# Two casts held behind a copy, gate sums and gate condition in longer runs of column products

## The chip, the core and the metric

The kernel runs on one core of one Trainium2 chip. The core has five engines that run beside each other and wait for each other through semaphores: TensorE (PE; PEld is its loading of weights), VectorE (DVE), ScalarE (ACT), GpSimd (POOL) and SyncE (SP), which here issues DMA transfers. Products are accumulated in banks of PSUM; everything else lies in SBUF or, between stages, in DRAM. The metric is the device time of one execution in microseconds, the median of several runs.

## The reference

One layer of a hybrid decoder, in float32, for a prompt of 1024 tokens and 8 samples of 4 tokens each, model width 1024:

```python
mod = jax.nn.silu(c) @ w_ada + b_ada
shift, scale, gate = jnp.split(mod, 3, axis=-1)
h = rmsnorm(x, g_norm) * (1 + scale[:, None, :]) + shift[:, None, :]
(mq, mk, mv, mi, mf, mo, mz, aq, ak, av, az, gm, ga) = split_in(h @ w_in)
y_m, C, n, m = mlstm_branch(mq, mk, mv, mi, mf, mo, mz, C0, n0, m0, b_i, b_f, g_mn)
o = sink_attend(q, k, v, q_pos, k_pos, sinks)
y_a = o * jax.nn.silu(az)
u = jax.nn.sigmoid(gm) * (y_m @ w_mo) + jax.nn.sigmoid(ga) * (y_a @ w_ao)
x = x + gate * (u @ w_o)
```

followed by a final rmsnorm. The outputs are the normed rows, the mLSTM state (C, n, m) and the kept keys and values, for prompt and samples. Three pieces of this matter here. The *gate sums* are the columns mi and mf of `h @ w_in`, 8 columns in all. The *gate condition* is the third part of `silu(c) @ w_ada`, called `gate`. The *job mk of head 0* is 128 columns of mk.

## The kernel before

**Exact products.** A float32 operand of the large products is split into hi and lo parts of a faster type (fp32r): `split4` (line 549) makes hi with an ACT copy, which the profile calls CAST, and lo with a DVE subtraction. A product is then three: hi x hi, hi x lo, lo x hi. Small products stay in plain float32 and are done on 32 columns of the array at a time: `mm(..., share=4)`, whose outputs go to the partitions 0, 32, 64 and 96 of one bank, four products beside each other. The profile shows full products as 128\*128 and column products as 128\*32.

**Jobs and pieces.** `job` (line 607) multiplies one block of 128 columns of the weights with all 1056 tokens, in three pieces of 384, 384 and 288 tokens (`PIECES`). Each piece is 24 products into one bank of the pair `pg` (`piece`, line 561), after which `evac` copies the bank out, on ACT for the jobs aq, mq and mk. With two banks, a piece has to wait for the copy of the piece two before it. At its start a job splits the weights of the next one (`prefetch`, which calls `split_weights`) and loads those of the one after that. The order is ak, av, aq0 to aq3, mq0, mk0, mv0, mq1; the other mLSTM jobs and all later ones are done in pairs by a scheme with fewer products, and there `split4` is called without `split_weights`. So the only job whose name begins with mk and which `split_weights` sees is mk0, at the start of mq0, when the three pieces of aq3 have been written down.

**Order.** Every PE instruction is chained to the one before it, so PE works in the order in which the program is written. On ACT and DVE (`S` and `V`, objects of the class `Ordered`, line 223) the same holds during the first stage, up to `V.on = S.on = False` (line 1985). After that the compiler's scheduler lays out each engine's order from the dependencies; `no_sync` adds a dependency that only fixes an order. Every engine runs its own queue in order. `Side` (line 113) is a planner, run while the program is written: it keeps a clock in estimated microseconds of PE work (`side.now`), and between products of a job it lets generators of side work take a step. A step ends with `yield lag, banks`: how long until the next visit, and which banks that needs.

**The stage around the gate sums** (lines 1925 to 1976). ak and av are made together, `pair` after `pair`, with four groups of two k blocks. In the last group, q = 3, stand: pair of pieces 0, its copies (`pair_end`), then the gate products for tokens 0 to 511 (`gate_piece(wg, zg, 0)`: 8 column products into the bank gg0, one ACT copy to zg0); pair of pieces 1, its copies, the first four sums (`gate_sums`: four small full products that add up the four partition groups of zg0 into gp), gate products 1; pair of pieces 2, its copies, sums four to seven from zg1, and gate products 2 for the 32 sample tokens. The ninth sum and all that depends on gp come later, as side work (`gates`). After that aq0 begins.

**The gate condition** is side work, `ada_gate` (line 1990). For each half of 512 columns it loads eight blocks of weights (adar_ga), and in two visits makes four column products each (`ada_products`, line 374); then DVE adds the bank's four groups to gb, and SP stores gb to DRAM.

Of the kernel before, what the change touches and what calls it, by code (L numbers as in the profile page):

```python
# [15 lines left out]
ALU = mybir.AluOpType  # L16
# [16 lines left out]
KT = D // 128  # L33
# [151 lines left out]
def body(tc, a):  # L185
    nc = tc.nc
    with ExitStack() as ctx:
# [34 lines left out]

        class Ordered:
            def __init__(self, eng, name):
                self.eng, self.name, self.on, self.late, self.before = eng, name, True, False, None

            def __getattr__(self, op):
                f = getattr(self.eng, op)

                def call(*args, **kw):  # L230
                    ins = f(*args, **kw)  # L231
                    i = getattr(ins, "ins", ins)
                    if self.on:
                        in_order(ins, self.name)
                    elif self.late and self.before is not None:
                        no_sync(i, [self.before])
                    self.before = i
                    return ins
                return call

        @contextmanager
        def not_before(*engs):
            for e in engs:
                e.late = True
            yield
            for e in engs:
                e.late = False

        V, S, G = Ordered(nc.vector, "V"), Ordered(nc.scalar, "S"), Ordered(nc.gpsimd, "G")
        G.on = False  # L250
# [302 lines left out]
            return hi, lo  # L553

        def split_weights(raws, name, eng):
            parts = [split4(raw, f"{name}_{i}", eng) for i, raw in enumerate(raws)]
            return tuple((lambda k, w=w: w[k // 4][:, k % 4]) for w in zip(*parts))

        banks = [pg]
# [1 line left out]
        def piece(w, rh, rl, kn, name, p, evac):  # L561
            wh, wl = w
            c0, n = PIECES[p]
            banks.append(banks.pop(0))
            acc = banks[-1]([128, 384], f"g_{name}{p}")
            o = acc[:, :n]
            for k in range(kn):
                mm(o, wh(k), rh(k, c0, n), start=(k == 0), stop=False)
                mm(o, wh(k), rl(k, c0, n), start=False, stop=False)
                mm(o, wl(k), rh(k, c0, n), start=False, stop=(k == kn - 1))  # L570
                if k < kn - 1:
                    side.tick()
            evac(p, acc, c0, n)
            side.tick()

        hs = {}

        def h_hi(k, c0, n, x="h"):
            ks = k
# [839 lines left out]
        class Pair:  # L1419
# [21 lines left out]
            def samples_end(self):  # L1441
                self.kind.samples(self, halves_sum(self.sums))

            def first_sums(self, behind=None):
                self.raw["s1"] = raw_tile("ws1")
                V.tensor_tensor(self.raw["s1"], self.raw[1, 0], self.raw[1, 1], op=ALU.add)
                if behind is not None:
                    no_sync(V.before, [behind])
                V.tensor_tensor(self.raw[1, 0], self.raw[0, 0], self.raw[1, 0], op=ALU.subtract)
                V.tensor_tensor(self.raw[0, 0], self.raw["s1"], self.raw[0, 0], op=ALU.subtract)  # L1450

# [118 lines left out]
        def block_products(jobs, hook):  # L1570
# [27 lines left out]
            for j, (n, i) in enumerate(flat):  # L1598
                job_ = jobs[n]
                nxt = jobs[n + 1] if n + 1 < len(jobs) else None  # L1600
                hook(n, i)
                if i == 3 and not nxt:
                    job_.samples_end()
                job_.kind.ahead(job_, i)
                if i == (5 if n else 6) and nxt:
                    nxt.load()
                split_ahead(j + 2)
                if i == 1:
                    o = NX = bank(pg, "bx")
                elif i == 5:  # L1610
                    o = Z = bank(pa, "bz")
                else:
                    o = {2: X, 3: W, 4: Y, 6: W, 7: Y}[i]
                new = i in (1, 5)
                wh, wl = job_.w.pop(i)
                for k in range(4):
                    bh, bl = blocks[OPERANDS[i]][k]
                    mm(o, wh[:, k], bh, start=(new and k == 0), stop=False, more=not new)
                    mm(o, wh[:, k], bl, start=False, stop=False, more=not new)
                    mm(o, wl[:, k], bh, start=False, stop=(k == 3), more=not new)  # L1620
                    if k < 3 and j:
                        side.tick()
                if i == 6:
                    Y = filled(pa, "by", W, n)
                elif i == 2:
                    job_.done(0, 0, X)
                    behind = job_.weighted if job_.kind is query_gate else None
                elif i == 5:
                    p5 = ht([128, 512], "p5")
                    S.copy(p5, Z)  # L1630
                elif i == 3:
                    job_.done(0, 1, p5, W)
                elif i == 4:
                    job_.done(1, 0, Y)
                if i == (7 if n else 5):
                    job_.done(1, 1, p5, Y)
                if i == (2 if n else 7) and nxt:
                    job_.samples_end()
                    nxt.samples()
                    side.free["b"] = side.now + HOLD["b"]  # L1640
                    side.tick(True)
                    if nxt.kind in (head_in, gate):
                        nxt.first_sums()
                if i == 7 and nxt and nxt.kind not in (head_in, gate):
                    nxt.first_sums(behind)
# [279 lines left out]
        for q, kk in enumerate(two):  # L1925
# [31 lines left out]
            if not more:  # L1957
                pair_end(0, acc[0])
                prefetch(order[2])
                zg = []  # L1960
                gate_piece(wg, zg, 0)
            if more:
                run(adas[q + 1])
            if q:
# [1 line left out]
            if more:  # L1966
                x_mul(1, kept[1], two[q + 1])
            else:
                pair_end(1, acc[1])
                gp = pb([128, 9, 8], "gp")  # L1970
                gate_sums(gp, zg, range(4))
                gate_piece(wg, zg, 1)
            pair(kk, 2, acc[2])
        pair_end(2, acc[2])
        gate_sums(gp, zg, range(4, 8))
        gate_piece(wg, zg, 2)
        for p, (c0, n) in enumerate(PARTS):
            if p == 2:
                dma(hD[:, :, SEQ:T], xS)
# [10 lines left out]
        def ada_gate():  # L1990
            for j in range(2):
# [454 lines left out]
```

## Time and profile before

| what | us |
| --- | --- |
| median of 3 runs (816.77 to 817.11) | 816.8 |
| the profiled execution | 816.58 |
| its span, first to last instruction | 814.8 |
| column products of the gate sums (gg) | 53.7 to 63.1 |
| column products of the gate condition (ada_ga) | 91.3 to 144.2 |
| casts of the weights of mk0 (wh_mk, two) | 123.1 to 124.2 |

The profile comes from one execution. Its span leaves out what lies before the first instruction and after the last, 1.78 us here. In the rows below, a row of the timeline is: start, duration, engine, line, operation, output <- inputs, shapes, count, and in brackets how long the engine had been idle and what ended that. A row of the list of waits is: total, times, longest. A row of the windows is: stretch, length, busy time with the count of instructions of PE, PEld, DVE, ACT and POOL, the granted clock of PE, the share of the DMA engines, GB/s. Matmuls overlap, so their durations say less than the distance from start to start.

### The profile page before, as it was taken

To read this page: it belongs to the slowest core of one execution; us is meant where nothing else is said; L and a number is where in the kernel's file an instruction comes from. 1 tells how busy PE (TensorE), PEld (TensorE's weight loads), DVE (VectorE), ACT (ScalarE), POOL (GpSimd) and SP (SyncE) were. 2 spreads that over 40 slices of the span, in tenths; PEclk is the share of its full clock that TensorE was granted. 3 is DMA by queue.
4 is the path that set the end of the run, shared out by engine and by line. 5 is a ranking of instruction groups with operands and counts; after the bars stand their busy time and mean duration, and the time that the engine had idled before them with its cause. 6 is when DMAs were issued, how large, how long until landed. Compare 5 with 4: busy or idle time off the path is not lost. (4 is left out here: it accounts for less than half of the span.)

```text
span 814.8 us, 15188 instructions
## 1 busy us (share of the span) xinstructions
PE 801.4 (98%) x5162; PEld 666.8 (82%) x5162; DVE 599.8 (74%) x1506; ACT 420.4 (52%) x1025; POOL 77.6 (10%) x156
## 2 busy tenths in 40 slices
PE   8999999999999999999999999999999999999996
PEld 5779888888788888888888888888888779997775
DVE  4899896755755557476668889898668997876666
ACT  5664356656565564546656555554446652224335
POOL 0120000010000000000001323231002101000000
PEclk9999999999999999999999999999999999999998
DMA  9994746646545424537764785864436589648622
GB/s 353 364 351 140 230 152 225 176 149 213 183 143 164 125 89 162 162 135 240 256 215 138 251 253 190 284 209 145 146 106 211 190 308 385 222 148 292 207 105 110
DMA packets 113218, 165.51 MB, mean 203 GB/s; under 512 B 21184, under 2 KB 55360, under 8 KB 113108
## 3 DMA queue, kind: packets, MB, share of 16 engines
q1 hardware_dynamic: 106740, 152.21, 56.2%
q10 hardware_dynamic: 4752, 7.60, 2.5%
q0 software_dynamic: 1648, 4.72, 1.5%
q8 instruction: 41, 0.67, 0.3%
q14 instruction: 37, 0.30, 0.1%
HBM read 115.51 MB, written 50.00 MB: 203 GB/s over the span
## 5 line engine op out<-in xcount | busy, mean ns | idle before, releaser
L231 ACT ACTIVATE p<-p,nmx 128x256 f32<-128x256 f32 (+1 forms) x64 | 31.1, 486 | 23.3 <-DVE nmx L231 23.2
L231 DVE CUSTOM_DVE_ANT_0 p<-sc,cst,sink 128x256 f32<-128x256 f32 (+1 forms) x64 | 26.1, 463 | 11.9 <-PE sc L286 11.8
L286 PE MATMUL g_aq<-h_h,wh_aq 128*128 128x384 f32 (+1 forms) x96 | 32.2, 336 | 0.0
L231 POOL TENSOR_SCALAR Cs<-Cs,sxb 128x129 f32<-128x129 f32 x32 | 27.6, 878 | 42.9 <-PE sn L286 42.9
L286 PE MATMUL g_aq<-h_h,wl_aq 128*128 128x384 f32 (+1 forms) x96 | 30.9, 322 | 0.0
L286 PE MATMUL g_aq<-h_l,wh_aq 128*128 128x384 f32 (+1 forms) x96 | 30.8, 321 | 0.0
L286 PE MATMUL g_w_mo<-ym_l,wh_w_mo 128*128 128x384 f32 (+1 forms) x96 | 30.8, 321 | 0.0
L286 PE MATMUL g_w_mo<-ym_h,wh_w_mo 128*128 128x384 f32 (+1 forms) x96 | 30.8, 321 | 0.0
L286 PE MATMUL g_w_mo<-ym_l,wl_w_mo 128*128 128x384 f32 (+1 forms) x96 | 30.8, 321 | 0.0
L272 POOL DMA_DIRECT2D oD<-uqv x16 | 8.7, 541 | 167.6 <-ACT uqv L231 167.6
L231 DVE COPY p<-pt 128x512 f32<-128x512 f32 (+1 forms) x16 | 10.5, 656 | 16.2 <-PE pt L291 16.2
L231 ACT CAST wosh<-wor 128x512 fp32r<-128x512 f32 x24 | 14.8, 621 | 13.8 <-DVE wor L231 13.0
L286 PEld LDWEIGHTS g_aq<-h_h,wh_aq 128*128 128x128 f32 x96 | 18.0, 188 | 2.5 <-issue 2.3
L231 DVE TENSOR_TENSOR wosl<-wor,wosh 128x512 fp32r<-128x512 f32 x24 | 16.5, 687 | 3.4 <-ACT wosh L231 3.2
L231 DVE SCALAR_TENSOR_TENSOR tgw_mo<-tgw_mo,g_w_mo 128x384 f32<-128x384 f32 (+1 forms) x24 | 12.4, 518 | 8.6 <-PE g_w_mo L286 6.8
L286 PE MATMUL g_mq<-h_h,wh_mq 128*128 128x384 f32 (+1 forms) x48 | 16.7, 348 | 1.6 <-ACT aq L231 1.2
L231 ACT ACTIVATE p<-p,den 128x256 f32<-128x256 f32 (+1 forms) x32 | 14.3, 490 | 7.6 <-DVE den L231 7.6
L286 PEld LDWEIGHTS g_aq<-h_l,wh_aq 128*128 128x128 f32 x96 | 18.1, 188 | 0.0
L286 PEld LDWEIGHTS g_w_mo<-ym_l,wh_w_mo 128*128 128x128 f32 x96 | 18.0, 188 | 0.0
L286 PEld LDWEIGHTS g_w_mo<-ym_h,wh_w_mo 128*128 128x128 f32 x96 | 18.0, 188 | 0.0
L286 PEld LDWEIGHTS g_w_mo<-ym_l,wl_w_mo 128*128 128x128 f32 x96 | 18.0, 188 | 0.0
L286 PEld LDWEIGHTS g_aq<-h_h,wl_aq 128*128 128x128 f32 x96 | 18.0, 188 | 0.0
(2068 smaller groups left out, 2827.6 us busy)
## 6 DMA issues: line engine op xcount, KB each, us to landing
early_h<-w_ada SPq DMA_DIRECT2D x8, 512.0 KB
adar_ga<-w_ada SPq DMA_DIRECT2D x16, 256.0 KB
wr_ga<-w SPq DMA_DIRECT2D x16, 256.0 KB
wr_gm<-w SPq DMA_DIRECT2D x16, 256.0 KB
taD<-gt SPq DMA_DIRECT2D x16, 256.0 KB
tmD<-gt SPq DMA_DIRECT2D x16, 256.0 KB
wor<-w_out SPq DMA_DIRECT2D x16, 256.0 KB
tga<-taD SPq DMA_DIRECT2D x16, 256.0 KB
```

The costliest lines, as they stand in the source:

```text
L231: ins = f(*args, **kw)
L272: ins = (eng or nc.sync).dma_start(out, in_)
L286: in_order(nc.tensor.matmul(out, lhsT, rhs, start=start, stop=stop, skip_group_check=more))
```

## The change

1. `split_weights` wraps the splits of a job whose name begins with mk in `behind(S, emptied)`: each ACT instruction made there gets an order dependency on `emptied`, the last ACT instruction of the latest evac. For mk0 that is the copy of the third piece of aq3.
2. The three gate pieces and the first eight gate sums are no longer put between the pairs of pieces, but all behind them; gp lies in a bank of the pair `pa` instead of `pb`.
3. In `ada_gate` the first of the two visits only advances the planner's clock and count as before; the second makes all eight column products of the half. So there are two runs of eight instead of four runs of four.
4. `first_sums` uses the new `behind` for an order that it recorded in another way before.

```diff
             def __init__(self, eng, name):
-                self.eng, self.name, self.on, self.late, self.before = eng, name, True, False, None
+                self.eng, self.name, self.on, self.late, self.before, self.behind = eng, name, True, False, None, []
...
                     elif self.late and self.before is not None:
                         no_sync(i, [self.before])
+                    no_sync(i, self.behind)
                     self.before = i
...
+        @contextmanager
+        def behind(e, others):
+            e.behind = list(others)
+            yield
+            e.behind = []
...
         def split_weights(raws, name, eng):
-            parts = [split4(raw, f"{name}_{i}", eng) for i, raw in enumerate(raws)]
+            with behind(S, emptied if name[:2] == "mk" else []):
+                parts = [split4(raw, f"{name}_{i}", eng) for i, raw in enumerate(raws)]
...
             evac(p, acc, c0, n)
+            emptied[:] = [S.before]
             side.tick()
...
-            def first_sums(self, behind=None):
+            def first_sums(self, others=()):
                 self.raw["s1"] = raw_tile("ws1")
-                V.tensor_tensor(self.raw["s1"], self.raw[1, 0], self.raw[1, 1], op=ALU.add)
-                if behind is not None:
-                    no_sync(V.before, [behind])
+                with behind(V, others):
+                    V.tensor_tensor(self.raw["s1"], self.raw[1, 0], self.raw[1, 1], op=ALU.add)
...
-                    behind = job_.weighted if job_.kind is query_gate else None
+                    gated_ = [job_.weighted] if job_.kind is query_gate else []
...
             if not more:
                 pair_end(0, acc[0])
                 prefetch(order[2])
-                zg = []
-                gate_piece(wg, zg, 0)
...
             else:
                 pair_end(1, acc[1])
-                gp = pb([128, 9, 8], "gp")
-                gate_sums(gp, zg, range(4))
-                gate_piece(wg, zg, 1)
             pair(kk, 2, acc[2])
         pair_end(2, acc[2])
-        gate_sums(gp, zg, range(4, 8))
-        gate_piece(wg, zg, 2)
+        zg, gp = [], pa([128, 9, 8], "gp")
+        for p in range(3):
+            gate_piece(wg, zg, p)
+        gate_sums(gp, zg, range(8))
...
                 acc = pb([128, 512], f"ada_ga{j}")
-                yield from ada_products(raws, acc)
+                side.now += 4 * 512 / 2400
+                side.products += 4
+                yield 2.0, "b"
+                was = side.now
+                for k in range(KT):
+                    c = 32 * (k % 4)
+                    mm(acc[c:c + 32], c32[:, k], raws[k], start=(k < 4), stop=(k >= 4), share=4)
+                side.now = was + 4 * 512 / 2400
+                yield 2.0, ""
```

More of the change, by code (lines that the diff above doesn't have):

```diff
@@ L573, in piece @@
             evac(p, acc, c0, n)
+            emptied[:] = [S.before]
             side.tick()
-        hs = {}
+        hs, emptied = {}, []
         def h_hi(k, c0, n, x="h"):
@@ L1644, in block_products @@
                 if i == 7 and nxt and nxt.kind not in (head_in, gate):
-                    nxt.first_sums(behind)
+                    nxt.first_sums(gated_)
                 if j == 0 or (i == 3 and nxt):
```

## Prediction

> **What bounds the kernel now.** I read the page's busy line first, then the list of waits on TensorE between 50 and 146 us (the stretch in which all the edits lie), then busy time by windows, and last the waits of VectorE and of the SP queue there.
>
> ```profile
> PE 801.4 (98%) x5162; PEld 666.8 (82%) x5162; DVE 599.8 (74%) x1506; ACT 420.4 (52%) x1025; POOL 77.6 (10%) x156
> ...
> PE g_mq L286 <- ACT aq L231: 1.2, 1, 1.2
> PE g_mq L286 <- ACT mk L231: 0.4, 1, 0.4
> ...
> 58.25:122.43 64.18, 62.98 (x438) 56.34 (x437) 58.81 (x194) 27.88 (x77) 2.73 (x6) 1.00 0.56 179
> 146.00:640.00 494.00, 493.63 (x3250) 409.19 (x3249) 348.82 (x871) 273.52 (x694) 60.06 (x123) 1.00 0.56 180
> ...
> DVE ropet L231 <- ACT aq L231: 1.5, 3, 0.8
> DVE gb L231 <- PE ada_ga L286: 1.2, 1, 1.2
> ...
> SPq L272 <- DVE gb L231: 7.6, 1, 7.6
> ```
>
> TensorE (PE) is busy 98% of the span, and from 146 to 640 us 493.63 of 494.00 us at full clock. So a microsecond taken from PE there, or before it, ends up in the total, unless something other than PE decides when PE reaches a later point. There is one such place: the wait of 1.2 us before g_mq. In the window that leads up to it, 58.25 to 122.43, VectorE (DVE) is busy 58.81 of 64.18 us, almost as tight as PE, while ScalarE (ACT) is busy 27.88. The next fence, from the timeline, shows how that window ends.
>
> ```profile
> 95.17 0.40 ACT L231 ACTIVATE p<-p,nmx 128x128 f32<-128x128 f32 x1 [4.89 <-DVE nmx L231]
> ...
> 117.03 0.29 PE L286 MATMUL g_aq<-h_h,wh_aq 128*128 128x288 f32 x1
> ...
> 118.11 0.51 ACT L231 ACTIVATE p<-p,nmx 128x256 f32<-128x256 f32 x1 [1.18 <-DVE nmx L231]
> ...
> 120.19 0.39 ACT L231 ACTIVATE gt<-gt,bcs 32x128 f32<-32x128 f32 x1
> ...
> 121.90 0.47 ACT L231 ACTIVATE aq<-g_aq 128x384 f32<-128x384 f32 x1
> ...
> 122.43 0.44 PE L286 MATMUL g_mq<-h_h,wh_mq 128*128 128x384 f32 x1 [1.20 <-ACT aq L231]
> 122.71 0.34 PE L286 MATMUL g_mq<-h_l,wh_mq 128*128 128x384 f32 x1
> 122.88 0.34 PE L286 MATMUL g_mq<-h_h,wl_mq 128*128 128x384 f32 x1
> ...
> 123.08 1.12 ACT L231 CAST wh_mk<-wr_mk 128x512 fp32r<-128x512 f32 x2
> ...
> 124.64 0.39 ACT L231 ACTIVATE aq<-g_aq 128x288 f32<-128x288 f32 x1
> ...
> 129.21 0.33 PE L286 MATMUL g_mq<-h_h,wh_mq 128*128 128x384 f32 x1
> ...
> 135.94 0.40 PE L286 MATMUL g_mq<-h_h,wh_mq 128*128 128x288 f32 x1 [0.38 <-ACT mk L231]
> ```
>
> The job aq3 has three pieces on two banks: piece 2 starts at 117.03, so piece 1 is complete by then, but ACT copies it out (128x384) only at 121.90, behind four exponentials that had waited for DVE's nmx until 118.11. PE's first g_mq needs that bank and starts at 122.43. So the time at which PE passes 122.43 is set by DVE's queue and ACT behind it, not by PE. ACT at 95.17 shows the same: 4.89 us of waiting for nmx.
>
> **Part 1, the held casts.** They are the two wh_mk casts at 123.08 (1.12 us together); the copy that they are held behind is that of aq3's last piece, 128x288, now at 124.64. The copy that PE waits for at 122.43 (at 121.90) is already ahead of the casts, so holding them cannot shorten the 1.2 us by itself. What it does is to bring the copy at 124.64 forward by up to 1.12 us. Its bank is wanted by g_mq's piece 1, which starts at 129.21: 4.2 us after the copy ends at 125.03. No PE time there. Queued behind the held casts are only the two DVE subtractions that make wl_mk; the first product that uses them comes after all three pieces of mq, the last of which starts at 135.94, so being late by the copy's 0.39 us costs nothing; without that cover it would be the 0.39 us. Bounds: a gain of 0.38, the wait at 135.94, if the subtractions leave DVE's queue before the softmax that delays mk's copy; a loss of 1.12 if the casts land right before that same copy. The nearest row is the 4.2 us of slack: I take **0**. The rewritten first_sums records the same dependency at the same instruction as before: nothing.
>
> **Part 2, the gate sums.** The rows are PE's, with the two of DVE and ACT that bear on the new order.
>
> ```profile
> 53.39 0.34 PE L286 MATMUL g_av<-h_l,wh_av 128*128 128x384 f32 x1
> 53.66 0.62 PE L286 MATMUL gg<-y,wg 128*32 128x512 f32 x2
> ...
> 54.17 0.69 DVE L231 TENSOR_TENSOR h_l<-x,h_h 128x512 fp32r<-128x512 f32 x1
> ...
> 55.52 0.44 PE L286 MATMUL g_ak<-h_h,wh_ak 128*128 128x384 f32 x1
> ...
> 55.70 0.59 ACT L231 COPY zg<-gg 128x512 f32<-128x512 f32 x1 [0.22 <-PE gg L286]
> ...
> 57.70 0.95 PE L286 MATMUL gp<-cst,zg 128*128 128x8 f32 x8
> ...
> 58.59 0.62 PE L286 MATMUL gg<-y,wg 128*32 128x512 f32 x2
> ...
> 62.13 0.95 PE L286 MATMUL gp<-cst,zg 128*128 128x8 f32 x8
> ...
> 62.49 0.62 ACT L231 CAST wh_aq<-wr_aq 128x512 fp32r<-128x512 f32 x1
> ...
> 63.01 0.33 PE L286 MATMUL gg<-small,wg 128*32 128x32 f32 x16
> ...
> 63.27 0.45 PE L286 MATMUL g_aq<-h_h,wh_aq 128*128 128x384 f32 x1
> ```
>
> And the gate condition (part 3), from PE's timeline too:
>
> ```profile
> 91.28 1.06 PE L286 MATMUL ada_ga<-adar_ga,c 128*32 128x512 f32 x8
> 92.28 0.45 PE L286 MATMUL g_aq<-h_h,wh_aq 128*128 128x384 f32 x1
> ...
> 95.09 1.07 PE L286 MATMUL ada_ga<-adar_ga,c 128*32 128x512 f32 x8
> 96.08 0.45 PE L286 MATMUL g_aq<-h_h,wh_aq 128*128 128x384 f32 x1
> ...
> 136.93 1.07 PE L286 MATMUL ada_ga<-adar_ga,c 128*32 128x512 f32 x8
> 137.93 0.40 PE L286 MATMUL g_mq<-h_h,wh_mq 128*128 128x288 f32 x1
> ...
> 143.72 1.07 PE L286 MATMUL ada_ga<-adar_ga,c 128*32 128x512 f32 x8
> 144.72 1.13 PE L286 MATMUL sc<-ukv,uqv 64*128 64x256 f32 x8
> ```
>
> First the price of going from full-width products (128*128) to products on 32 columns (128*32) and back. Four column products take 1.00 us (91.28 to 92.28); the gate's eight take 1.86 (53.66 to 55.52). So each four cost 0.86 and each run has 0.14 that is not products. The last full product before a run starts 0.27 ahead of it (53.39 to 53.66), against 0.17 between neighbours (122.71 to 122.88): 0.10 more. The first full product after a run or a wait takes 0.28 (122.43 to 122.71): 0.11 more. **One run costs 0.35 us beside its products**, of which 0.25 on the way out.
>
> Before, from 53.56 (53.39 plus 0.17), when the second pair of pieces could have started, to the first g_aq at 63.27 are 9.71 us. Pair 1 takes 2.18 (55.52 to 57.70), of which 0.11 is the restart; the eight sums 0.89 (57.70 to 58.59) and again 0.88 (62.13 to 63.01); gate piece 1 and pair 2 together 3.54 (58.59 to 62.13), so pair 2 is 3.54 less 1.86, or 1.68, again with 0.11; the small gate piece 0.26. After the change the same work is: pair 1 2.07, pair 2 1.57, way in 0.10, sixteen column products 3.44, small piece 0.26, way out 0.05 to 0.14, sixteen sums 1.77. That is 9.26 to 9.35, a saving of 0.36 to 0.45; I take **0.45** at this place.
>
> The covers that go: gate piece 0 hid DVE's last h_l (54.17, done at 54.86). Pair 1 now starts at 53.56 and needs that h_l for its last two products, at 53.56 + 10 x 0.17 = 55.3: still 0.4 in hand. ACT's copies of the gates were hidden by a pair of pieces. Now the copy of gate piece 1 starts when its products end, near 60.7, plus the 0.18 that the first one took after its run (55.52 to 55.70), and takes 0.59: done at 61.5. The small piece and the first half of the sums (0.26 + 0.89) keep PE busy to 61.9. Covered by 0.4, unless two aq casts of 0.62 (as at 62.49) are put ahead of it: then 0.8 is lost. The sums' bank moves to the other pair of banks, whose last user is copied out by about 58; nothing waits. No DMA is issued by the moved steps; only the K stores come due a little sooner in the planner's clock.
>
> **Part 3, the gate condition in two runs.** The first four products of each half move into the visit of the second four; the planner's clock advances as before, so PE's other work keeps its order. Half 0: the run at 91.28 stands behind score products and goes whole, 1.00 less; the second grows by 0.86: **0.14** saved. Half 1: the run at 136.93 stood between full products, so 1.00 + 0.10 + 0.10 goes (its return has 288-wide products, 0.10 more), against 0.86: **0.34** saved. The second runs end no later than now, so gb's additions on DVE and SP's store of it, for which SP waits 7.6 us, are not delayed. The cost is memory: four 512-column tiles of the common pool live from 91.28 to 95.09, and from 136.93 to 143.72, longer. Nothing in the trace prices that; bounds are 0 and the 0.38 of one more wait like that at 135.94. I take 0.
>
> [...]
>
> **The sum.** Of the 0.59 saved ahead of 122.43 (0.45 + 0.14), PE merely arrives earlier at a copy whose time DVE sets. DVE's work ahead of it is unchanged, and only about 0.2 of its idle time there (part of the 1.2 that gb waits for PE) gets shorter without the next wait, for ACT's aq, growing. So 0.2 passes (bounds 0 and 0.59) and the 1.2 us wait grows to about 1.6. Of the 0.34 after it all passes, since PE is full from 146 on. 0.2 + 0.34 = 0.54: the profiled execution's 816.58 us (span 814.8 and 1.78 around it) becomes 816.04. The median of the runs shown, 816.8, is 0.22 higher, which gives **816.3 us** as the measured time.
>
> **The rivals.** *A, the wait goes too.* The order of ACT and DVE is laid out at compile time by list scheduling (only PE's order is written by hand), and the edits shift it. If aq's copy is put ahead of the softmax that it now follows, the 1.2 us goes and all of 0.59 + 0.34 counts: 2.1 less, 814.7. For it: piece 1 is complete at 117.03, and ACT idles 1.18 us before 118.11. Against: no edit touches that copy.
> *B, slower.* The same order falls the other way: one more group of exponentials, 2.08 us on ACT (118.11 to 120.19), comes ahead of the copy at 121.90. That copy has no slack, so every microsecond counts in full from the first: 816.3 + 2.08 = 818.4. For it: four tiles live longer and the held casts change what ACT finds ready. Against: the group's own tiles are the scarcer.
> *C, nothing arrives.* The gains are given back: the 0.59 in the grown wait, the rest in the gate copies (0.8 exposed) or in one more 0.38: 816.8. [...] Here each copy is 0.59 against 1.72 of products, so the rows speak against it.
>
> **How the numbers follow.** Forecast 0.50 (its own range 815.5 to 817.1: all of the 0.59 passing and the 0.38 of part 1 gained, or the 0.8 of the gate copies lost), A 0.22, B 0.13, C 0.15. The bound of 0.2% is 1.63 us, about what a measurement of this kernel can tell from no change: faster means under 815.2, slower over 818.4. Faster: A nearly whole, 0.21, and 0.06 from the forecast's edge: 0.27. Slower: half of B and a little for other orders: 0.10. Same: 0.63. The range runs from 814.3, a little under A, to 818.2, most of the way to B.
>
> **What would show it.** Right: one block of gg and gp rows just before the first g_aq, which starts 0.4 to 0.5 earlier; two ada_ga groups of 1.86 instead of four of 1.00; the two wh_mk casts behind the 128x288 aq copy; the g_mq wait at 1.2 to 1.7. Part 2 is wrong if a wait of PE on ACT zg shows. Wrong altogether if that g_mq wait is gone (A) or over 3 us (B), or if a new PE wait of over 0.5 us appears between 60 and 146 us.

## The result and the profile after

The changed kernel takes **820.66 us** (median of 5, 820.36 to 822.89) where the kernel before takes 816.77 beside it: ratio 1.0055, interval [1.0044, 1.0067]. It is slower, by 3.9 us; the forecast was 816.3, in a range of 814.3 to 818.2. The profiled execution took 820.36 with a span of 818.6 (before: 816.58 and 814.8).

First the busy line of the page after the change, and the list of waits on TensorE between 50 and 170 us (total, times, longest), the views with which the prediction began:

```profile
PE 803.6 (98%) x5162; PEld 669.3 (82%) x5162; DVE 599.1 (73%) x1506; ACT 420.3 (51%) x1025; POOL 77.5 (9%) x156
```

```profile
PE g_mk L293 <- ACT mk L231: 3.8, 1, 3.8
PE g_mq L293 <- ACT mk L231: 0.4, 1, 0.4
PE g_ak L293 <- DVE h_h L231: 0.3, 1, 0.3
```

The wait of 1.2 us for aq is gone, and a new one of 3.8 has come: mk0's first piece waits for the copy of mq0's second. The instructions are the same in number, yet PE is busy for 2.2 us more. The windows of the same stretch tell why (stretch, length, busy PE, PEld, DVE, ACT, POOL, granted clock, DMA share, GB/s):

```profile
138.00:140.00 2.00, 0.74 (x7) 0.43 (x3) 0.00 (x0) 0.37 (x1) 0.00 (x0) 1.00 0.61 153
140.00:142.00 2.00, 0.00 (x0) 0.00 (x0) 1.46 (x5) 2.00 (x7) 0.00 (x0) 0.65 0.68 241
142.00:144.00 2.00, 1.44 (x4) 1.44 (x5) 1.51 (x3) 2.00 (x7) 0.37 (x1) 0.50 0.38 142
144.00:146.00 2.00, 2.00 (x10) 1.50 (x13) 0.69 (x1) 0.54 (x2) 0.17 (x1) 0.50 0.52 167
146.00:148.00 2.00, 2.00 (x16) 0.32 (x8) 0.00 (x0) 0.37 (x1) 0.00 (x0) 0.65 0.26 70
148.00:150.00 2.00, 2.00 (x19) 1.23 (x12) 1.68 (x3) 0.56 (x2) 0.42 (x1) 1.00 0.14 25
```

The granted clock falls to 0.5 during the wait and stays there when PE has work again; the trace's clock records put it at 0.5 from 140.58 to 147.41. PE's timeline shows both halves of the loss, and that PE was ahead of before up to the wait:

```profile
133.66 0.40 PE L293 MATMUL g_mq<-h_h,wh_mq 128*128 128x288 f32 x1 [0.38 <-ACT mk L231]
...
142.56 0.69 PE L293 MATMUL g_mk<-h_h,wh_mk 128*128 128x384 f32 x1 [3.81 <-ACT mk L231]
143.04 0.52 PE L293 MATMUL g_mk<-h_l,wh_mk 128*128 128x384 f32 x1
143.36 0.52 PE L293 MATMUL g_mk<-h_h,wl_mk 128*128 128x384 f32 x1
...
145.74 2.73 PE L293 MATMUL ada_ga<-adar_ga,c 128*32 128x512 f32 x16
148.39 0.49 PE L293 MATMUL sc<-ukv,uqv 64*128 64x256 f32 x2
```

mq0's third piece starts at 133.66, 2.28 ahead of the 135.94 of before. Of this, 0.23 is not the change's: PE is that much ahead at 53.16 (53.39 before), in front of the first edited step, and the profiles of all runs scatter there from 0.21 behind to 0.76 ahead, with and without the edits. Behind the wait, full products stand 0.32 apart instead of 0.17. The account: 2.28 ahead, and 1.20 more because the run of 1.00 that stood between the products of that piece is gone (with its way in and back), makes 3.48 ahead; the wait takes 3.81; half 1's run has four products more, 0.86; and from 142.56 to 147.41 PE works at half clock, which costs half of 4.85, 2.4. Sum: 3.6 behind. Measured at sc: 148.39 against 144.72, 3.67; at the end of the span 3.8.

What ends the wait shows in ScalarE's timeline of the changed kernel, up to the copy that PE wants:

```profile
133.13 0.48 ACT L231 ACTIVATE mk<-g_mq 128x384 f32<-128x384 f32 x1
133.63 0.37 ACTq L279 DMA_DIRECT2D qD<-mk  x1
...
139.63 0.62 ACT L231 CAST t3h<-x 128x512 fp32r<-128x512 f32 x1 [3.47 <-DMA qD<-mk]
140.15 0.40 ACT L231 ACTIVATE p<-p,nmx 128x128 f32<-128x128 f32 x1
...
141.50 0.62 ACT L231 CAST wh_mv<-wr_mv 128x512 fp32r<-128x512 f32 x1
142.02 0.48 ACT L231 ACTIVATE mk<-g_mq 128x384 f32<-128x384 f32 x1
```

and in the kernel before:

```profile
138.01 0.62 ACT L231 CAST t3h<-x 128x512 fp32r<-128x512 f32 x1 [0.59 <-PE ada_ga L286]
...
139.04 0.47 ACT L231 ACTIVATE mk<-g_mq 128x384 f32<-128x384 f32 x1
```

t3h is a cast of the later block scheme (`sum_blocks`), which PE first uses at 219.8. It waits for a store to land, everything behind it on ACT waits too, and in that queue stands the copy that frees mk0's bank. The store is that of mq0's first piece: t3h's tile gets the buffer of that piece. In the built programs the waits recorded for two tiles of the common pool (`ht`, 50 buffers, line 205) are:

```
                          before                        after
t3h, fourth block         PE, first run of half 1       DMA qD<-mk, mq0's first piece
mk, mq0's second piece    PE, first run of half 1       DMA qD<-aqr, aq3's third piece
```

Before, both take buffers of weight tiles (adar_ga) that the first run of half 1 has read. In the changed kernel those four tiles are held until the second visit, and the next buffers in turn are of tiles that a store still reads.

### The profile page after: what moved, and what is told of

Same layout as the page of the kernel before. It is cut to its first block, busy times and chain, and to the rows that moved or that the text cites. A ratio compares the mean times of both kernels' runs of the same rounds, so it can differ in the third digit from the quotient of the medians.

```text
span 818.6 us, 15190 instructions
## 1 busy us (share of the span) xinstructions
PE 803.6 (98%) x5162; PEld 669.3 (82%) x5162; DVE 599.1 (73%) x1506; ACT 420.3 (51%) x1025; POOL 77.5 (9%) x156
## 5 line engine op out<-in xcount | busy, mean ns | idle before, releaser
L293 PE MATMUL sc<-ukv,uqv 64*128 64x256 f32 (+1 forms) x128 | 17.9, 390 | 0.0
```

The costliest lines, as they stand in the source:

```text
L293: in_order(nc.tensor.matmul(out, lhsT, rhs, start=start, stop=stop, skip_group_check=more))
```

## Experiments

**Theory M (memory):** the four tiles held longer send t3h to a buffer that a store frees late; the wait and the low clock follow. **Rivals:** the held casts or the moved sums shift ACT's order (R1); the long run on PE itself makes the stage late (R2).

| run | kernel | median, us | before beside it | ratio, interval |
| --- | --- | --- | --- | --- |
| e1 | parts 1 and 2 | 817.96 | 816.39 | 1.0015 [1.0006, 1.0024] |
| e2 | part 3 | 820.30 | 816.39 | 1.0021 [1.0000, 1.0042] |
| e3 | all, half 1 in two runs, tiles held | 818.66 | 816.39 | 1.0026 [1.0015, 1.0037] |
| e4 | all, runs at the first visit | 814.72 | 816.39 | 0.9981 [0.9972, 0.9989] |
| e5 | part 1 | 816.56 | 816.27 | 0.9999 [0.9990, 1.0008] |
| e6 | part 2 | 816.91 | 816.27 | 1.0008 [0.9999, 1.0017] |
| e7 | all, half 1 as before | 814.28 | 816.27 | 0.9979 [0.9970, 0.9988] |
| e8 | part 3, runs at the first visit | 814.72 | 816.27 | 0.9979 [0.9971, 0.9988] |
| e9 | half 0 of part 3 | 814.73 | 816.32 | 0.9983 [0.9974, 0.9992] |
| e10 | all, half 1 at the first visit | 814.47 | 816.32 | 0.9978 [0.9969, 0.9987] |
| e11 | e10 without part 2 | 814.98 | 816.32 | 0.9985 [0.9976, 0.9994] |
| e12 | e7, gate sums twice | 819.25 | 816.32 | 1.0036 [1.0023, 1.0048] |
| e13 | all, one store's source altered | 814.41 | 816.69 | 0.9972 [0.9962, 0.9982] |
| e14 | all, three stores' source altered | 815.85 | 816.69 | 0.9990 [0.9981, 0.9999] |
| e15, e16 | part 3 again, one execution each | 820.07, 821.37 | 816.69 | |
| e17 | all, one store earlier | 815.73 | 816.41 | 0.9991 [0.9982, 0.9999] |
| e18 | all, one store from SP | 814.57 | 816.41 | 0.9982 [0.9974, 0.9991] |

### Which part: e1, e2, e5, e6

e1 leaves part 3 out:

```diff
-                side.now += 4 * 512 / 2400
-                side.products += 4
...
+                yield from ada_products(raws, acc)
```

> Parts 1 and 2 without part 3: half 0 and half 1 of the gate condition in two runs each, as before. Theory M (memory): with part 3 the four tiles adar_ga of half 1 are held until the second visit, so the cast t3h gets a buffer whose store (qD<-mk) is still landing, ACT's queue stands behind it, the copy of mk comes 3.8 us late for PE's first g_mk, and PE then runs at a granted clock of 0.5 for some us. Without part 3 that wait is gone; what the changed kernel had gained by 133.66 (g_mq's third piece 2.28 us earlier than before) less the 0.14 of half 0 stays: 816.8 - 2.1 = 814.6, no PE wait over 0.5 us between 130 and 150. Rival R1 (the held casts or the moved gate sums shift ACT's order, and the wait is theirs): the wait of g_mk for mk stays, 819 or more.

e2 makes part 3 alone (the diff of the change without the hunks of `split_weights` and the gate sums):

> Part 3 alone: the casts not held, the gate sums as before, both halves of the gate condition in one run each. Theory M: t3h waits for the store as in the changed kernel, g_mk waits 3 to 5 us for mk, the granted clock falls to 0.5 behind it, and as parts 1 and 2 bring nothing here, the kernel is slower than the changed one by up to 2: 820 to 823. Rival R1 (the wait belongs to parts 1 or 2): 816.3 (0.14 + 0.34 saved), no wait of g_mk over 0.5.

The waits of PE, first in e1, then in e2:

```profile
PE g_mq L293 <- ACT aq L231: 0.9, 1, 0.9
PE g_mq L293 <- ACT mk L231: 0.4, 1, 0.4
```

```profile
PE g_mk L293 <- ACT mk L231: 3.8, 1, 3.8
PE g_mq L293 <- ACT mk L231: 0.4, 1, 0.4
```

The new wait comes and goes with part 3, as M said; R1 falls. Two things M did not say. e1 is not 814.6: the old wait is back and the gain is gone with it, so **most of what the changed kernel had gained by the third piece is part 3's too**. And e2's twelve executions fall into two groups, 814.6 to 815.3 (five) and 820.1 to 822.3 (seven): the same program gains or loses. Its profile is of the second group, and so is its median; the ratio of 1.0021 comes from all twelve and lies between the groups.

e5 is part 1 alone and e6 part 2 alone:

```diff
+            with behind(S, emptied if name[:2] == "mk" else []):
```

```diff
-                gate_sums(gp, zg, range(4))
-                gate_piece(wg, zg, 1)
...
+        for p in range(3):
+            gate_piece(wg, zg, p)
+        gate_sums(gp, zg, range(8))
```

> Part 1 alone, the two wh_mk casts held behind the copy of aq's last piece. Theory M: nothing arrives, within 0.3 of before; the copies at 121.9 and g_mq at 122.43 stay where they are, g_mk waits for nothing. Rival R3 (the held casts themselves cost): the 128x288 copy earlier, but wl_mk or the copy of mk later, 0.4 to 1.1 more than before.

> Part 2 alone, the gate sums in one run. [...] So between 0 and +1.5, with more spread than before's. Rival R4 (the gain passes, no loss): 0.45 to 0.8 less than before, spread as before's.

e5 is the kernel before to within its interval, so R3 falls. PE's timeline and PE's waits in e6:

```profile
62.44 0.42 PE L293 MATMUL g_aq<-h_h,wh_aq 128*128 128x384 f32 x1
```

```profile
PE g_mq L293 <- ACT aq L231: 1.2, 1, 1.2
```

The first g_aq starts 0.83 ahead of the 63.27 of before, but 0.43 of that was there at the last product of the first pair of pieces, ahead of the moved sums. From that product to the first g_aq PE takes 9.48 us in e6 and 9.45 in the changed kernel, where it took 9.88: part 2 saves 0.40 to 0.43. From the first g_aq to g_mq it takes 59.18 (59.16 before). So the wait for aq did not grow, and the 0.40 passes the place where the prediction let most of it end. PE is still 0.75 ahead at 650 us and loses 0.5 there, where it waits 0.2 for wl_ao1A (0.9 in e1); e5 loses 0.4 at the same place. In time e6 gains nothing, so R4 falls: eight executions lie from 816.35 to 817.16 and three from 818.03 to 818.63. The +1.5 of the expectation is near what e1 shows behind the gate sums: a spell of granted clock 0.5 of 3.41 us near 64 (the windows stand under e12), by which PE is 1.54 later there.

### Memory or the long run: e3, e4, e7

e3 puts half 1 back into two runs but holds the four tiles by leaving 8 columns of each first product to the second visit:

```diff
+                    for k in range(4):
+                        mm(acc[32 * k:32 * k + 32, 8:], c32[:, k], raws[k][:, 8:], start=True, stop=False, share=4)
+                    yield 2.0, "b"
+                    for k in range(4):
+                        mm(acc[32 * k:32 * k + 32, :8], c32[:, k], raws[k][:, :8], start=False, stop=False, share=4)
```

> The changed kernel with half 1 of the gate condition in two runs as before, but of the first run's four products the last 8 of 512 columns (here columns 0 to 7) are left to the second visit, so that the four weight tiles stay held as in the changed kernel. Theory M: t3h still waits for the store, g_mk waits 3 to 5 us: 819.5 to 821.5. Rival R2 (it is the long run of column products on PE that makes the stage late, not the memory): wait gone, 814.6 to 815.

e4 keeps the long runs and moves them to the first visit, so that nothing is held:

```diff
-                side.now += 4 * 512 / 2400
-                side.products += 4
-                yield 2.0, "b"
                 was = side.now
                 for k in range(KT):
...
                 side.now = was + 4 * 512 / 2400
+                yield 2.0, "b"
+                side.now += 4 * 512 / 2400
+                side.products += 4
                 yield 2.0, ""
```

> The changed kernel, but the one run of eight column products of each half is made at the first of the two visits instead of the second, so that all eight tiles come free at the first. Theory M: t3h's buffer is free in time, no wait of g_mk over 0.5, both savings of part 3 stay: 816.8 - 2.28 - 0.34 = 814.2. Rival R2 (the long run itself): g_mk or its copy late by the run's 0.86 or more, 816 to 820. Should a weight tile land after the first visit, PE would wait at ada_ga instead, in sight in the list of waits.

e7 is the changed kernel with half 1 as before (`ada_products` for j == 1):

```diff
+                if j == 0:
...
+                else:
+                    yield from ada_products(raws, acc)
```

> The changed kernel, but half 1 of the gate condition in two runs as before; only half 0 is made in one. Theory M with what the other runs showed: the wait of g_mq for aq at 122.43 goes because half 0's late run lets DVE do the rope of aq before gb's additions (DVE waited 1.16 + 0.57 there), 1.8 to 2.1 less than before, and t3h's buffer is free, no wait of g_mk: 814.3 to 815, with some executions 1.5 longer for a spell of half clock near 64. Rival R5 (the 2 us come from half 1, or from parts 1 and 2 only together with half 1): 816.4 or more and the wait at 122.43 stays.

Held without the long run, the wait is there (e3, the list of waits of PE and the timeline of ACT); the long run without holding has none (e4, e7 list no wait of g_mk):

```profile
PE g_mk L293 <- ACT mk L231: 2.1, 1, 2.1
```

```profile
139.02 0.62 ACT L231 CAST t3h<-x 128x512 fp32r<-128x512 f32 x1 [3.08 <-DMA qD<-mk]
```

R2 falls: e4 and e7 gain where e3 loses, and only e3 holds tiles. R5 falls with e7. e3's wait is 2.1, not the 3 to 5 expected: half 1's first run stands between the products again, so that PE comes to g_mk 1.0 later than in the changed kernel (measured against before), and the store lands 0.6 earlier (t3h at 139.02 against 139.63). Its time of 818.66 is 0.8 under the lower end expected.

### Where the gain is: e8, e9, e10, e11

e9 is half 0's run alone (the new code for j == 0, `ada_products` for j == 1), e8 is e4's edit without parts 1 and 2:

> Half 0 of the gate condition in one run and nothing else of the change. Theory M: DVE no longer stands behind gb's first addition at 95, the wait of g_mq for aq at 122.43 goes, 1.1 to 1.8 less than before. Rival R7 (it takes the moved gate sums too to get the wait away): within 0.3 of before, the wait at 122.43 stays.

> Part 3 alone, with each half's run of eight at the first visit; casts not held, gate sums as before. Theory M: the wait of g_mq for aq goes as with the late run, t3h's buffer is free in time, and without the run of gate sums there is no spell of half clock near 64: 1.8 to 2.3 less than before (814.1 to 814.6 where before has 816.4), spread as narrow as before's. Rival R6 (parts 1 and 2 have a share in the gain): less than 1.2 gained.

e9 alone removes the wait for aq and takes 1.6 us less than before, e8 1.55, which is a little under what was expected; R6 and R7 fall. DVE's waits from 90 to the start of g_mq (122.43 and 120.24) say how, before and then in the changed kernel:

```profile
DVE ropet L231 <- ACT aq L231: 1.5, 3, 0.8
DVE gb L231 <- PE ada_ga L286: 1.2, 1, 1.2
DVE p L231 <- PE pt L291: 0.7, 1, 0.7
DVE t2l L231 <- ACT t2h L231: 0.2, 1, 0.2
```

```profile
DVE den L231 <- ACT p L231: 1.1, 1, 1.1
DVE bcs L231 <- PE bq L293: 0.8, 1, 0.8
DVE p L231 <- PE pt L298: 0.4, 1, 0.4
```

DVE's first gb addition stood at the head of its queue and waited 1.16 us for half 0's second run, and the rope of aq's piece behind it. With one run the compiler's order puts that rope first:

```profile
94.41 0.59 DVE L231 STREAM_SHUFFLE ropet<-aq 128x384 f32<-128x384 f32 x1
95.03 0.56 DVE L231 TENSOR_TENSOR ropet<-ropet,sin 128x384 f32<-128x384 f32 x1
95.51 0.55 DVE L231 TENSOR_TENSOR aq<-aq,cos 128x384 f32<-128x384 f32 x1
95.98 0.67 DVE L231 TENSOR_TENSOR gb<-ada_ga,gb 9x512 f32<-9x512 f32 x1
```

Its waits for aq and ada_ga are gone, the exponentials at 118.11 start at 115.47, and ACT copies aq out at 119.27 instead of 121.90, before PE needs the bank at 120.24. PE's timeline of the changed kernel:

```profile
62.61 0.42 PE L293 MATMUL g_aq<-h_h,wh_aq 128*128 128x384 f32 x1
...
120.24 0.33 PE L293 MATMUL g_mq<-h_h,wh_mq 128*128 128x384 f32 x1
```

From the first g_aq to g_mq are 57.63 us, 1.53 less than before; in e9, with the gate sums as before, 57.66. With the runs at the first visit (e4, e8) they are 58.01.

e10 makes half 0's run at the second visit and half 1's at the first; e11 is that without part 2:

```diff
+                if j == 0:
                     side.now += 4 * 512 / 2400
                     side.products += 4
                     yield 2.0, "b"
...
+                if j == 1:
+                    yield 2.0, "b"
+                    side.now += 4 * 512 / 2400
+                    side.products += 4
```

> The changed kernel with half 0's run of eight at the second visit (as changed) and half 1's at the first. Theory M: 2.26 less (as with half 0 merged only) and 0.34 more for half 1's shorter way: 2.6 less than before, 813.7, in some executions 1.5 longer for the spell of half clock near 64. Rival R2 (a long run of column products costs in half 1's stage whenever it is made): 814.3 or more.

> As the run before it, but with the gate sums as before the change. Theory M: 1.4 to 2.0 less than before, no execution with a spell of half clock near 64, so a narrower spread. Rival R8 (the spread comes from elsewhere): a group of executions 1.5 longer here too.

e10's 814.47 is 0.8 over what was expected, which was R2's sign. But PE gains 0.11 across half 1 there (1.05 ahead of before at the third piece of g_mq, 1.16 ahead after both visits), so the long run itself costs nothing; the 0.34 expected is the price of the late place. Its times and those of e4 and e7 are alike, and e11's are no narrower than e10's, so R8 holds: not all of the spread of such kernels is the spell near 64. With part 2 the ratio is lower by 0.0004 (e7 against e9) and 0.0007 (e10 against e11), less than the intervals tell apart.

### What ends the wait: e13 to e18

> The changed kernel, but the store of mq's first piece (qD<-mk, 128x384) takes its data from a tile of h instead of the copied-out piece, so that the DMA is the same and t3h's buffer is free at once; what is stored for mq there is not mq. The weight tiles stay held, the runs stay at the second visit. In the built program the copy of mq's second piece still gets a buffer that a store frees (qD<-aqr, which landed at 139.8 in the changed kernel). Theory M (a landing of a store ends the wait): the wait for qD<-mk goes, the copy goes at 139.8 instead of 142.02, g_mk waits 1.2 to 2.0 instead of 3.8, at most one spell of 3.41 us at half clock: 815.5 to 818.5. Rival R10 (the place of mk's copy in ACT's queue, behind the exponentials and casts, makes the wait, not the landing): g_mk waits 3 or more, 820.

> As the run before it, and the stores of aq3's second and third piece (qD<-aqr) take their data from the same tile of h: neither t3h nor the copy of mq's second piece stands behind a landing then, with the same DMAs, the weight tiles held and the runs late as in the changed kernel; what is stored there is not aq. Theory M: no wait of g_mk over 0.5, all gains stay: 2.3 + 0.34 less than before, 813.6 to 814.3 where before has 816.3, some executions 1.5 longer for a spell near 64. Rival R2 (the long late run) or R10 (ACT's queue): a wait of g_mk stays, 816 or more.

```diff
-                    issue(dst[:, c0:c0 + m], t[:, :m], eng=nc.scalar)
+                    from_ = h_hi(0, 0, 384).bitcast(F32) if scale != 1.0 and h == 0 and p == 0 else t
+                    issue(dst[:, c0:c0 + m], from_[:, :m], eng=nc.scalar)
```

In both the wait of g_mk is gone although the tiles are held and the runs are late, so R2 falls once more. The runs changed more than was meant, though: the altered store no longer depends on mq and went out at 70 us, so that the DMA near 134 was not the same, and e13's other store landed in 2.7 us, not 6.1; besides, PE came 1.1 later than in the changed kernel, behind a spell at 63.04. So e13's g_mk does not wait the 1.2 to 2.0 expected, and its 814.41 is better than the range. ACT's order moved too: t3h now stands ahead of the exponentials. Against R10 speaks the changed kernel's own timeline, where ACT stands idle for 3.47 us until the store lands, rather than these two runs. e14's 815.85 is 1.5 over what was expected; its profile shows new waits of 0.6 for wl_ao1A and 0.3 for uqv. (What e13 and e14 store there is not mq, and in e14 not aq either.)

Part 3 alone again, for a profile of either of its groups:

> Part 3 alone once more, for its profile: 5 of its 12 executions took 814.6 to 815.3, 7 took 820.1 to 822.3. Theory M: which of the two is set by when the store qD<-mk lands; with a time near 815 the wait of t3h for it is under 1 us and g_mk does not wait, near 821 both waits are over 3 us and the granted clock falls to 0.5 behind them. Rival R11 (the two groups differ in the clock alone): the same waits in both.

> The same kernel a second time, to have a profile of either group: as for the first look.

Both are of the slower group (waits of g_mk 3.7 and 3.9), so that R11 stays open. But the trace's records of the semaphores tell, for every profile, when the 16 reports of a store came. These are the sixteen profiles with both stores near 134 (in e13 and e14 the store from ACT went out at 70), as pairs of qD<-mk (ACT's queue) and qD<-aqr (SP's):

```
                        issued      apart   qD<-mk landed after   its last 8 reports
before                  135.92       0.74          6.59            4.5 after the first 8
after                   133.63       0.07          5.97            3.6
e1, e2, e3, e4, e5      133.4-136.3  0.04-0.74     4.72-5.97       2.9-4.0
e7, e8, e10, e11, e12   133.4-138.2  0.05-0.85     5.06-6.26       3.1-4.1
e15, e16                133.9-134.2  0.33-0.39     5.82-6.10       3.9-4.1
e6                      135.13       1.57          2.81            none
e9                      133.89       1.72          2.88            none
```

So the store lands late in the kernel before as well, at 142.5; nobody waited for it. It is late where the two stores are issued within 0.9 us of each other, and not in the two profiles where they are 1.6 and 1.7 apart. SP's store is as late wherever it comes second (8 of 8: before, after, e2, e7, e8, e11, e15, e16; 6.2 us after its issue before, 6.1 in the changed kernel) and lands in 2.7 to 2.9 where it comes first (6 of 6). Hence theory L, tested by issuing mq's first store from SP too:

```diff
-                    issue(dst[:, c0:c0 + m], t[:, :m], eng=nc.scalar)
+                    issue(dst[:, c0:c0 + m], t[:, :m], eng=None if scale != 1.0 and h == 0 and p == 0 else nc.scalar)
```

> The changed kernel with the store of mq's first piece issued by SP instead of ACT. In 14 of 16 profiles the two stores, qD<-mk from ACT and qD<-aqr from SP, were issued within 0.9 us of each other and qD<-mk landed 4.7 to 6.6 us after its issue, the last 8 of its 16 reports 3 to 4.5 us behind the first 8; in the two with 1.6 and 1.7 us between them both landed in 2.6 to 2.9. Theory L (the late landing comes from two queues' stores meeting): here SP issues both, over 0.9 us apart, both land in 2.6 to 3.2, no wait of g_mk over 1, 813.7 to 815. Rival R13 (it lies in the place or the time): the 8 late reports stay.

SP's queue and ACT's in e18:

```profile
133.23 0.32 SPq L279 DMA_DIRECT2D qD<-mk  x1
...
134.95 0.33 SPq L279 DMA_DIRECT2D qD<-aqr  x1
```

```profile
137.05 0.61 ACT L231 CAST t3h<-x 128x512 fp32r<-128x512 f32 x1
...
138.05 0.48 ACT L231 ACTIVATE mk<-g_mq 128x384 f32<-128x384 f32 x1
```

The stores land 1.8 and 2.7 us after issue, t3h waits for nothing, g_mk waits 0.2, and the kernel takes 814.57: the whole change, with one store's queue altered, beats both kernels. In the built program t3h still takes the buffer of mq's first piece and still waits for its store; it just has landed in time, at 135.0. That is as theory L said, and R13 falls. But the two stores are also 1.7 apart here, so that the run does not tell the queue from the distance. And the gain is not due to the landing alone: the copy of mq's second piece got a buffer that no store reads, and t3h stands later in ACT's order.

e17 asks whether a pool as full is harmless once these stores are out of the way:

```diff
-            due.append((side.now + 8.0, out, in_))
+            due.append((side.now + lag, out, in_))
...
+                store(dram[:, c0:c0 + m], dst[:, :m], 5.0 if dram is qD[3] and c0 == PIECES[2][0] else 8.0)
```

> The changed kernel with one number altered: the planner's delay for the store of aq3's third piece (qD<-aqr) is 5 us instead of 8, so that SP issues it near 123 instead of 133.7, its tile comes free by then, and in the built program neither t3h nor the copy of mq's second piece takes a buffer that a store near 134 frees. Held tiles, late runs and ACT's order of t3h ahead of mk's copy stay. Theory M: no wait of g_mk over 0.5, 2.3 to 2.6 less than before: 813.7 to 814.5 where before has 816.5, some executions 1.5 longer for a spell near 64. Rival R12 (another buffer or queue makes the same wait, as the pool is as full as in the changed kernel): g_mk waits over 1, 817 or more.

ACT's timeline and PE's waits in e17:

```profile
142.26 0.62 ACT L231 CAST t4h<-x 128x512 fp32r<-128x512 f32 x1 [1.78 <-DMA qD<-mk]
```

```profile
PE pt L298 <- DVE gb L231: 1.2, 1, 1.2
```

g_mk no longer waits, but the next cast of that scheme, t4h, now takes the buffer of the next store and waits 1.78, and PE waits 1.2 for gb a little later. 815.73: the held tiles moved the wait on rather than out (R12 in part). Half 1 in two runs (e7, 0.9979), or at the first visit (e4, e10, 0.9981 and 0.9978), has neither wait; these beat both kernels.

### The clock behind small products: e12

> The changed kernel with half 1 in two runs and the first eight gate sums computed twice, one after the other, so that the stretch of 8-column products behind the gate pieces is 3.6 us long instead of 1.8. If such a stretch counts as idle for the clock gate, nearly every execution has a spell of 3.41 us at half clock right after it: 1.8 for the products and 1.5 to 1.7 for the spell on top of half 0 merged only, 817.4 to 817.9 where that had 814.3, and granted clock 0.5 between 63 and 69. Rival R9 (small products keep the clock up; the spells have another cause): 816.1, spells as rare as before.

```diff
         gate_sums(gp, zg, range(8))
+        was = side.now, side.products
+        gate_sums(gp, zg, range(8))
+        side.now, side.products = was
```

The windows of e1 and then of e12, behind the gate sums:

```profile
62.00:64.00 2.00, 2.00 (x16) 1.73 (x16) 2.00 (x6) 0.08 (x1) 0.00 (x0) 0.99 0.00 0
64.00:66.00 2.00, 2.00 (x8) 2.00 (x7) 2.00 (x10) 1.10 (x3) 0.00 (x0) 0.50 0.30 104
66.00:68.00 2.00, 2.00 (x9) 2.00 (x9) 2.00 (x4) 1.99 (x4) 0.00 (x0) 0.66 0.91 280
```

```profile
62.00:64.00 2.00, 2.00 (x15) 2.00 (x14) 2.00 (x5) 0.00 (x0) 0.00 (x0) 0.69 0.00 0
64.00:66.00 2.00, 2.00 (x9) 2.00 (x10) 0.70 (x3) 0.00 (x0) 0.00 (x0) 0.50 0.00 0
66.00:68.00 2.00, 2.00 (x9) 1.54 (x9) 1.01 (x5) 0.38 (x2) 0.00 (x0) 0.50 0.03 8
```

PE is busy all the time, and the clock falls to 0.5 all the same: from 63.96 for 3.41 us in e1, from 62.75 for 6.83 in e12. e12's five executions all lie over 817.8. Of the twelve profiles with part 2, four (e1, e10, e12, e13) have such a spell, which begins between 62 and 64; of the eight without it, none. So sixteen sums of 8 columns in a row, 1.8 us, bring the spell about in some executions, and 3.6 us, by the five times, in all; R9 falls. e12's time is 1.35 over the range expected; in its profile the spell is twice as long as expected and PE waits 0.9 near 650.

## Why the prediction was wrong, point by point

- **What bounds the kernel.** Right that DVE and ACT set the time at 122.43. Wrong that hence only 0.2 of PE's earlier arrival passes: in e6 all of part 2's 0.40 passes with the wait unchanged. DVE's work hangs on copies of PE's products (rope waits for ACT's aq) and moves with them. e1 shows the same the other way round: the spell near 64 makes PE 1.54 later there, and g_mq comes 1.20 later, with a wait only 0.3 shorter.
- **Part 1**, taken as 0: e5 measures 0.9999 [0.9990, 1.0008].
- **Part 2**, 0.45 at the place: 0.43 in the changed kernel and 0.40 in e6, so the term was right. No wait for zg appears; the covers held. The half-clock spell behind the run of sums (3.41 us in e1, PE 1.54 later) was not foreseen; it stands in four of the twelve profiles with part 2. In time e6 has no gain; how much of that is the spell and how much the stage near 650 is open.
- **Part 3's own saving**, 0.14 and 0.34: in the changed kernel PE goes from 0.69 to 0.83 ahead across half 0, so 0.14. Across half 1, made late as predicted and without the wait, e17 goes from 2.51 to 2.81 and e14 from 1.90 to 2.21, so 0.30 and 0.31. These terms were right too.
- **Part 3 and DVE.** The prediction counted 0.2 of the 1.2 that gb waits for PE. Measured, half 0's run took the wait for aq away altogether: from the first g_aq to g_mq the changed kernel takes 1.53 less, where the prediction had 0.14 for half 0 and 0.4 back for a longer wait. This is rival A's gain, which had 0.22, by a way not named: DVE's queue, not the place of one copy.
- **The step that failed** is part 3's memory: "four 512-column tiles of the common pool live from 91.28 to 95.09, and from 136.93 to 143.72, longer. Nothing in the trace prices that; bounds are 0 and the 0.38 of one more wait like that at 135.94. I take 0." It cost 3.81 of waiting and, as an estimate from half of 4.85, 2.4 of half clock. The upper bound was the wait of a kernel in which those four buffers came free in time. The trace had a sign of it: `t3h` before waits for ada_ga (0.59 at 138.01), that is, for just the first run that the change removes, with PE's copy next but one behind it on ACT.
- **Rival B** named the four tiles that live longer as its reason and had the right kind of place, a copy late in ACT's queue, but at aq's copy, through the order and for 2.08; it was mq's copy, through a buffer and for 3.81. Two of the signs that the prediction named came: the wait of g_mq gone (A), and a new wait of PE between 60 and 146.

The spells of half clock last 3.41 us (e1, e3, e10, e13, e15) and 6.83 us (the changed kernel, e2, e12, e16). The clock fell with PE idle in the changed kernel (at 140.58, a wait of 3.81 us) and in e3 (at 141.73, a wait of 2.15), and in e1 at 63.96 with no idle time of PE. What sets the start and the length of a spell, and whether small products count as idle there, as e12's expectation supposed, no run shows.

## What to carry to other kernels

When a change holds tiles of a shared pool longer, look up in the timeline who waits for those tiles to be read (here t3h for ada_ga) and ask whose buffer that instruction gets next; if a store reads it, the price is the store's landing and all that stands behind the instruction on its in-order queue (here 3.47 us of ACT's time and 3.81 of PE's), not nothing. Merge small products where the weights come free early: at the first visit (e4, 0.9981), or with the half whose buffers nobody takes (e7, 0.9979). A stretch of very small products can be followed by a lower clock as a wait can (e1: sixteen sums of 8 columns, 1.8 us, then clock 0.5 for 3.41 us); and a wait of 2.1 to 3.9 us, with the half clock behind it, cost 1.4 to 1.8 times its length here (an estimate from e3, e15, e16 and the changed kernel, half of the time worked at half clock added to the wait).

## What was not expected of the hardware

A store issued on ACT's queue within 0.9 us of one on SP's told of its landing 4.7 to 6.6 us after issue, eight of its sixteen reports 2.9 to 4.5 us behind the others, and SP's store likewise where it came second; 1.6 us or more apart each landed in 1.8 to 2.9. Why half of the reports are late is open. Part 3 alone has two groups of times, 814.6 to 815.3 and 820.1 to 822.3; that this landing decides between them is likely, but there is no profile of the faster group. Granted clock 0.5 was seen without any idle time of PE, behind 1.8 us of products of 8 columns (3.6 in e12), in four of twelve profiles; what decides in which is open.
